# Hybrid SSM and attention layer: the attention stage's transfers in the written order

## Chip, cores and metric

The kernel runs on one core of one Trainium2 chip. The metric is the device time of one execution in microseconds. The engines are named as in the profile: PE is TensorE, DVE VectorE, ACT ScalarE, POOL GpSimd, SP SyncE (here it issues nearly all transfers).

## The reference

The reference is one layer: a pre-norm whose result feeds a state-space group and an attention group, an output projection, and a gated feed-forward part (2048 tokens of 1024 features, float32).

```python
h = rmsnorm(x, norm_mix_g[l])
proj = h @ w_in[l]                      # u_ssm (512) | q (512) | k (512) | v (512)
y_ssm = s5_mixer(u_ssm, ...)            # 32 groups of 16 channels, complex diagonal state of 64
y_att = chunked_attention(q, k, v, rel_bias)   # 8 heads of 64; own 64-token chunk and 8 before it
mixed = concatenate([rmsnorm(y_ssm, g_s), rmsnorm(y_att, g_a)])
x = x + mixed @ w_out[l]
h2 = rmsnorm(x, norm_ffn_g[l])
x = x + (silu(h2 @ w_gate[l]) * (h2 @ w_up[l])) @ w_down[l]
return rmsnorm(x, norm_final_g)
```

## The kernel before

A float32 product is made of three matmuls (`mm3`): each operand is split into a rounded high part (`hi`, `wh`) and the remainder (`lo`, `wl`), and hi by hi, hi by lo and lo by hi are added in PSUM. The stages follow one another: the SSM's input projection (`u_phase`, up to about 125 us), attention with the SSM as filler (about 143 to 731 us), mixing and output projection (from about 687 us), gate and up, and down (from about 1860 us).

The attention stage runs over 128 steps: 4 blocks of 512 tokens (`sb`), 4 pairs of heads, 2 heads, 4 query tiles. A step issues scores (`scores`: `sc`, with the mask tile `nb` added on DVE and the row minimum `mn`), the transposes of an earlier step (`transp`: `pt`, copied by ACT into `pth` and its remainder by DVE into `ptl`), the product with v at the end of a head (`pv_head`, `pv_scale`: `ya`, stored into `ya_s`), and then matmuls of "units", generators that are advanced a little in each step:

- `hT_unit` makes the normalised input tiles of a block, eight of them, q0 to q7. A tile `xt` is loaded into one of XB = 2 buffers, scaled on DVE, cast to `hi` by ACT and subtracted into `lo` by DVE (`low`). For blocks 1 to 3, q0 to q2 and q3 to q7 are two units, started 12 and 8 steps ahead of the block's first step.
- `qk_unit` and `v_unit` project q, k and v (`pf`). In block 0 their weights are loaded as `raw`, split into a hi and lo tile, and kept in DRAM (`keep_w`: `wss`). Later blocks load the split weights back (`w<-wss`, 1024 KB each) into WB = 3 buffers. q's two parts go to `q2h` and `q2l`, which are copied to the other half of the partitions by a transfer each. k's go to the right half of `k2`. The left half holds the keys of the block before, which were kept in DRAM (`ks`) and are loaded back.
- `ssm_unit` does four groups of SSM: U, Bst, Tm and Vm are loaded (18 transfers), products on PE, a scan on POOL, and y is stored in eight transfers (`y<-X`). Unit b starts at step 2 + 15 b.

A unit's loads are issued in the program two or three steps ahead of its matmuls. PE's order is the written one (`Ordered`). On the other engines a scheduler orders the instructions by its own priorities, except those issued through `Pinned` (`k.V`, `k.A`, `k.Q`), which it keeps in the order of the program among themselves on their engine. An instruction that waits on SP holds up all transfers that stand behind it. Tiles are named with a running number (`raw_2605`), which the order rows below show; in the profile the number is left out.

Of the kernel before, what the change touches and what calls it, by code (L numbers as in the profile page):

```python
# [78 lines left out]

class Pinned:  # L80


    def __init__(self, tc, eng):
        self.tc, self.eng = tc, eng

    def __getattr__(self, name):
        f = getattr(self.eng, name)
        return lambda *a, **b: self.tc.keep_in_program_order(f(*a, **b))


class K:
    def __init__(self, tc, io):
        self.tc, self.nc, self.io = tc, tc.nc, io
        self.n = 0
        self.te = Ordered(tc)
        self.ta = self.te if PINA else tc.nc.tensor
        self.V, self.A, self.Q = (Pinned(tc, e) for e in (tc.nc.vector, tc.nc.scalar, tc.nc.sync))
# [462 lines left out]
def ssm_unit(k, p, psum, S, b, eng):  # L560

    nc = k.nc
    F = GB * CH
    U = k.t(p, "U", [P, GB, NC])

    def load(out, in_):
        ins = nc.sync.dma_start(out, in_)
        if b == 0:
            k.tc.keep_in_program_order(ins)

    for j in range(L):
        load(U[j * CH : (j + 1) * CH], S["u"][b * F : (b + 1) * F, j, :].rearrange("(g c) t -> c g t", c=CH))
    gs = slice(GB * b, GB * b + GB)
    bst = k.t(p, "Bst", [P, GB, P])
    load(bst[:].rearrange("p g m -> p (g m)"), S["bst"][b // 2][:, (b % 2) * GB * P : (b % 2 + 1) * GB * P])
    tm = k.t(p, "Tm", [P, GB, P])
    for i in range(L):
        load(tm[i * CH : (i + 1) * CH], S["kt"].rearrange("c g a m -> c g (a m)")[:, gs, P - CH * i : 2 * P - CH * i])
    vm = k.t(p, "Vm", [P, GB, P])
    load(vm[:], S["v"].rearrange("q g c n m -> (c n) (q g) m")[:, gs, CH:])  # L580
    for _ in range(YL):
        yield

    X = k.t(p, "X", [P, 2, GP, NC])
    for q in range(GP):
        ps = k.t(psum, "pj", [P, 2, NC], bufs=2)
        for g2 in range(2):
            k.ta.matmul(ps[:, g2, :], bst[:, 2 * q + g2, :], U[:, 2 * q + g2, :], start=True, stop=True)
        for g2 in range(2):
            for c in range(2):  # L590
                nc.scalar.copy(X[g2 * NS : (g2 + 1) * NS, c, q, :], ps[c * NS : (c + 1) * NS, g2, :])  # L591
        yield

    a8 = S["a8"]
    qs = slice(GP * b, GP * b + GP)
    Xk = X[:].rearrange("p r q (k s) -> p r q k s", s=8)
    Xe = Xk[:, :, :, :, 7].rearrange("p r q (a b) -> p r q a b", b=8)

    def step(dst, src, e, n):

        ar = a8[:, 0, qs, (0, 7, 15)[e]].unsqueeze(1).to_broadcast([P, 2, GP]).unsqueeze(3).to_broadcast([P, 2, GP, n])
        aw = S["sw"][:, e, :, qs].unsqueeze(3).to_broadcast([P, 2, GP, n])
        t = k.t(p, "st1", [P, 2, GP, NC // 8])
        t2 = k.t(p, "st2", [P, 2, GP, NC // 8])
        eng.tensor_tensor(t[:, :, :, :n], src, ar, op=ALU.mult)  # L605
        eng.tensor_tensor(t2[:, :, :, :n], src[:, ::-1], aw, op=ALU.mult)
        eng.tensor_tensor(dst, dst, t[:, :, :, :n], op=ALU.add)
        eng.tensor_tensor(dst, dst, t2[:, :, :, :n], op=ALU.add)

    def carry(dst, end, i0, n):  # L610

        for c in range(2):
            for e in range(2):
                t = k.t(p, "fx", [P, GP, NC // 8, 7])[:, :, :n]
                pw = a8[:, c if e == 0 else 1 - c, qs, i0 : i0 + 7].unsqueeze(2).to_broadcast([P, GP, n, 7])
                eng.tensor_tensor(t, end[:, e].unsqueeze(3).to_broadcast([P, GP, n, 7]), pw, op=ALU.mult)
                eng.tensor_tensor(dst[:, c], dst[:, c], t, op=ALU.subtract if e == 1 and c == 0 else ALU.add)
            yield

    for s in range(1, 8):  # L620
        step(Xk[:, :, :, :, s], Xk[:, :, :, :, s - 1], 0, NC // 8)
        yield
    for b_ in range(1, 8):
        step(Xe[:, :, :, :, b_], Xe[:, :, :, :, b_ - 1], 1, 4)
        yield
    for a in range(1, 4):
        step(Xe[:, :, :, a : a + 1, 7], Xe[:, :, :, a - 1 : a, 7], 2, 1)
        yield
    yield from carry(Xe[:, :, :, 1:, :7], Xe[:, :, :, :3, 7], 8, 3)
    yield from carry(Xk[:, :, :, 1:, :7], Xk[:, :, :, : NC // 8 - 1, 7], 0, NC // 8 - 1)  # L630

    if b == 0:
        k.XG = k.t(p, "XG", [P, GB, NC])
        nc.gpsimd.memset(k.XG[:, :, 0:1], 0.0)
    XG = k.XG
    XGv = XG[:].rearrange("p (q g) c -> p q g c", g=2)
    for g2 in range(2):
        for c in range(2):
            eng.dma_start(XGv[c * NS : (c + 1) * NS, :, g2, 1:], X[g2 * NS : (g2 + 1) * NS, c, :, : NC - 1])
    for _ in range(YX):  # L640
        yield
    Y = k.t(p, "X", [P, GB, NC])
    for q in range(GP):
        ps = k.t(psum, "pj", [P, 2, NC], bufs=2)
        for g2 in range(2):
            g = 2 * q + g2
            k.ta.matmul(ps[:, g2, :], tm[:, g, :], U[:, g, :], start=True, stop=False)
            k.ta.matmul(ps[:, g2, :], vm[:, g, :], XG[:, g, :], start=False, stop=True)
        nc.scalar.copy(Y[:, 2 * q : 2 * q + 2, :], ps[:])
        if q == GP - 1:  # L650
            for j in range(L):
                nc.sync.dma_start(S["y"][b * F : (b + 1) * F, j, :].rearrange("(g c) t -> c g t", c=CH), Y[j * CH : (j + 1) * CH])
        yield


# [25 lines left out]
def att_phase(k, ident, S):  # L681
    tc, nc, io = k.tc, k.nc, k.io
    with ExitStack() as cx:
# [3 lines left out]
        def load_w(sb, n):  # L687

            w = k.t(aw, "w", [P, 2, 1024], F32R, bufs=WB)
            if sb == 0:  # L690
                raw = k.t(aw, "raw", [P, 1024], bufs=2)
                pin = n in (0, 4)
                (k.Q if pin else nc.sync).dma_start(raw[:], io["w_qk"][n] if n < 8 else io["w_v"][n - 8])
                split(k, w[:, 0], w[:, 1], raw[:], k.V if pin else k.wlo_eng, k.A if pin else None)
                keep[n] = w
            else:
                nc.sync.dma_start(f32(w[:]), S["ws"][n])
            return w[:, 0], w[:, 1]

        def keep_w(n):  # L700
            if n in keep:
                (k.Q if n in (0, 4) else nc.sync).dma_start(S["ws"][n], f32(keep.pop(n)[:]))

        def hT_unit(sb, q0=0, q1=KT):
            hi, lo = hT.setdefault(sb, ([], []))
            ts = slice(sb * SB, (sb + 1) * SB)
            xts = {}
            V, A, Q = (k.V, k.A, k.Q) if sb == 0 else (nc.vector, nc.scalar, nc.sync)

            def load(q):  # L710
                if q < q1:
# [9 lines left out]

            for q in range(q0, q1):
                yield
                load(q + ahead)
                xt = xts[q]
                for v, n in zip(hT[sb], ("hi", "lo")):
                    v.append(k.t(aw, f"{n}{q}x" if q < DB and sb % 2 else f"{n}{q}", [P, SB], F32R))
                V.scalar_tensor_tensor(xt[:], xt[:], k.gm[:, q : q + 1], S["rsn"][:, ts], op0=ALU.mult, op1=ALU.mult)
                A.copy(hi[q][:], xt[:])  # L729
                if sb == 0 and q:  # L730
                    low(q - 1)
                if sb or q == KT - 1:
                    low(q)
            yield

        def qk_unit(sb, pr):
# [5 lines left out]
            else:  # L742
                ts = [(k.t(aa, "q2h", [P, SB], F32R, bufs=3), k.t(aa, "q2l", [P, SB], F32R, bufs=3), k.t(aa, "k2", [P, 2 * SB], F32R, bufs=3)) for _ in range(2)]
            qk[sb, pr] = ts
            if sb > 0:
                for hh in range(2):
                    nc.sync.dma_start(f32(ts[hh][2][:, :SB]), S["k"][(sb - 1) % 2, 2 * pr + hh])
            both = (sb, pr) == (0, 0)
            pss = []
            for c in range(2):  # L750
# [13 lines left out]
                for hh in range(2):  # L764
# [3 lines left out]
                    if c == 0:  # L768
                        nc.scalar.activation(q2h[a, :], ps[a, :], AF.Copy, scale=-0.125)
                        nc.vector.scalar_tensor_tensor(q2l[a, :], ps[a, :], -0.125, f32(q2h[a, :]), op0=ALU.mult, op1=ALU.subtract)  # L770
                        nc.sync.dma_start(f32(q2h[o, :]), f32(q2h[a, :]))
                        nc.sync.dma_start(f32(q2l[o, :]), f32(q2l[a, :]))
                    else:
                        nc.scalar.copy(k2[a, -SB:], ps[a, :])
                        nc.vector.tensor_tensor(k2[o, -SB:], ps[a, :], f32(k2[a, -SB:]), op=ALU.subtract)
                        if sb < NSB - 1:
                            nc.sync.dma_start(S["k"][sb % 2, 2 * pr + hh], f32(k2[:, -SB:]))
                yield

        QK_N = 1 + 2 * KT  # L780
# [33 lines left out]

        def load_nb(h):
            nb = k.t(aa, "nb", [P, 640], bufs=2)
            nc.sync.dma_start(nb[:], S["nbm"][h])
            return nb

        def scores(st):  # L820
# [70 lines left out]
        def pv_scale(st):  # L891
# [4 lines left out]
            for i in range(4):  # L896
                k.ta.transpose(pb[:, i * P : (i + 1) * P], rb[:, i].rearrange("p h d -> p (h d)"), ident[:])
            nc.vector.tensor_tensor(ya[:], ya[:], pb[:], op=ALU.mult)
            nc.sync.dma_start(S["ya"][sb, pr * P : (pr + 1) * P, :], ya[:])

        st_head, yas, sums, rbs = {}, {}, {}, {}
        steps = [(sb, pr, hh, qp) for sb in range(NSB) for pr in range(4) for hh in range(2) for qp in range(4)]
# [43 lines left out]
        N = len(steps)  # L946
        for s in range(N + LAG + 2):
            if s == OPEN:
                aw.release()
                mix = mix_phase(k, S, lambda: k.t(pfs, "pf", [P, 512]))  # L950
                units += [Unit(islice(mix, MIX_N), MIX_N, GSTART, N + LAG, GSTART - OPEN)]
# [753 lines left out]
```

## Time and profile before

| | |
|---|---|
| median of 3 runs | 2314.3 us (2306.25 to 2315.94) |
| the profiled execution's own time | 2304.9 us |
| its span | 2303.1 us |
| its mean granted PE clock | 0.975 |
| PE busy in the span | 2183.8 us, 95% |
| transfers | 437 MB, 190 GB/s in the mean |

The profile is of one execution; its span runs from the first to the last instruction. A row of a timeline gives start, duration, engine, line, operation, and output and inputs; in brackets stand the idle time of the engine before it and what ended that. SPq is SP's queue, whose rows are transfers being issued; the row ends with the issue, and the transfer lands some microseconds later. The rows of transfers give the count, the KB of one and the median time from issue to landing.

### The profile page before, as it was taken

How to read it: one execution, taken by the hardware profiler on the slowest of the kernel's cores; microseconds unless marked ns; L12 is line 12 of the kernel's file. 1: busy time of each engine (PE TensorE's matmuls, PEld its weight loads, DVE VectorE, ACT ScalarE, POOL GpSimd, SP SyncE). 2: the span in 40 equal slices, each digit the busy share in tenths (PEclk: the TensorE clock that was granted, in tenths of full speed). 3: DMA queues.
4: the chain of work that ended last, by engine and by line, in shares of the span. 5: the costliest groups of instructions: out<-in, count | busy, mean ns of one | idle time of the engine just before them, and what ended most of it. 6: DMA issues, size and time to landing. Idle time of an engine off the chain costs nothing.

```text
span 2303.1 us, 30454 instructions
## 1 busy us (share of the span) xinstructions
PE 2183.8 (95%) x10568; PEld 1834.1 (80%) x10568; DVE 1487.8 (65%) x2286; ACT 1001.3 (43%) x1675; POOL 1061.0 (46%) x1245
## 2 busy tenths in 40 slices
PE   8978799999997899989999999999999999999997
PEld 6667688898986788778888887888888878888886
DVE  7845555656555756676775669766645376578676
ACT  6335555555557542343333335333333343344332
POOL 3416655455660433265555554555555314445442
PEclk9989999999998999999999999999999999999998
DMA  8788766766653534754554556555433287465552
GB/s 295 260 286 265 235 210 204 207 190 193 192 137 114 178 118 163 249 165 143 167 193 157 205 190 254 195 193 167 158 96 110 76 326 265 165 228 183 201 182 74
DMA packets 216370, 437.00 MB, mean 190 GB/s; under 512 B 27352, under 2 KB 58120, under 8 KB 209112
## 3 DMA queue, kind: packets, MB, share of 16 engines
q1 hardware_dynamic: 211352, 420.89, 55.0%
q0 software_dynamic: 4864, 14.17, 1.9%
q8 instruction: 83, 1.36, 0.2%
q14 instruction: 71, 0.58, 0.1%
HBM read 294.98 MB, written 132.15 MB: 185 GB/s over the span
## 4 chain that ended last, share of the span: by engine, by line
PE 59%; DVE 3%; DMA 1%; ACT 1%; issue 1%; POOL 1%; SPq 0%; DVEq 0%; ACTq 0%; POOLq 0%
PE X L74 20%; PE ps L74 18%; PE Y L74 10%; PE big L74 6%; PE W L74 5%; DVE acc L1575 1%; DMA lo<-hc 0%; DMA x<-xt 0%; DVE xt L1117 0%; DVE lo L166 0%; DVE hd L166 0%; POOL c L166 0%; ACT hi L165 0%; POOL sa L1125 0%; DMA gl<-x 0%
## 5 line engine op out<-in xcount | busy, mean ns | idle before, releaser
L74 PE MATMUL X<-hi,c 128*128 128x512 f32 x1408 | 452.2, 392 | 7.6 <-ACT u L1391 3.5
L74 PE MATMUL ps<-hd,hd 128*128 128x512 f32 (+1 forms) x1968 | 431.7, 381 | 3.9 <-DVE hd L166 3.7
L74 PEld LDWEIGHTS ps<-hd,hd 128*128 128x128 f32 x1968 | 358.8, 190 | 75.5 <-DVE hd L166 5.1
L166 POOL TENSOR_TENSOR c<-S,c 128x512 fp32r<-128x512 f32 x176 | 253.1, 1440 | 260.7 <-ACT c L165 258.8
L74 PEld LDWEIGHTS X<-hi,c 128*128 128x128 f32 x1408 | 265.8, 189 | 65.2 <-ACT u L1391 5.1
L74 PE MATMUL X<-lo,c 128*128 128x512 f32 x704 | 275.3, 391 | 0.0
L166 POOL TENSOR_TENSOR hd<-hd 128x1536 fp32r<-128x1536 f32 (+1 forms) x46 | 159.1, 3463 | 232.0 <-ACT hd L165 218.8
L166 POOL TENSOR_TENSOR c<-raw,c 128x512 fp32r<-128x512 f32 x132 | 189.0, 1432 | 137.5 <-ACT c L165 109.1
L165 ACT CAST hd<-hd 128x1536 fp32r<-128x1536 f32 (+1 forms) x106 | 147.4, 1393 | 219.4 <-DMA hd<-hq 134.5
L74 PE MATMUL Y<-hi,c 128*128 128x512 f32 x704 | 225.5, 391 | 4.8 <-DVE u L1395 4.8
L1521 DVE TENSOR_TENSOR acc<-acc,ps 128x512 f32<-128x512 f32 x196 | 129.2, 681 | 79.5 <-PE ps L74 79.1
L74 PE MATMUL big<-m,woh 128*128 128x512 f32 x512 | 165.4, 404 | 0.6 <-DVE m L166 0.4
L165 ACT CAST c<-S 128x512 fp32r<-128x512 f32 x176 | 109.5, 622 | 116.5 <-PE Y L74 59.1
L74 PE MATMUL pf<-hi,w 128*128 128x512 f32 x416 | 150.9, 415 | 9.4 <-ACT hi L729 5.8
L74 PEld LDWEIGHTS Y<-hi,c 128*128 128x128 f32 x704 | 132.6, 188 | 33.9 <-DVE u L1395 6.3
L74 PEld LDWEIGHTS X<-lo,c 128*128 128x128 f32 x704 | 133.0, 189 | 27.7
L1391 ACT COPY u<-X 128x512 f32<-128x512 f32 x132 | 77.1, 585 | 177.5 <-PE X L74 177.5
L846 DVE CUSTOM_DVE_ANT_0 s<-sc,nb 128x640 f32<-128x640 f32 (+4 forms) x128 | 94.4, 737 | 89.4 <-PE sc L74 85.9
L605 POOL TENSOR_TENSOR st<-X,a 128x128 f32<-128x128 f32 (+2 forms) x136 | 47.4, 349 | 220.0 <-ACT X L591 157.4
L165 ACT CAST c<-raw 128x512 fp32r<-128x512 f32 x132 | 82.1, 622 | 143.1 <-PE Y L74 80.3
L166 DVE TENSOR_TENSOR hd<-hd 128x1536 fp32r<-128x1536 f32 (+1 forms) x60 | 119.3, 1990 | 31.2 <-ACT hd L165 30.5
L74 PE MATMUL Y<-lo,c 128*128 128x512 f32 x352 | 137.2, 390 | 0.0
(462 smaller groups left out, 4644.2 us busy)
## 6 DMA issues: line engine op xcount, KB each, us to landing
w<-wss SPq DMA_DIRECT2D x36, 1024.0 KB, 5.5
hq<-g SPq DMA_DIRECT2D x140, 256.0 KB, 2.1
hd<-hq SPq DMA_DIRECT2D x42, 768.0 KB, 4.5
hd<-wc SPq DMA_DIRECT2D x42, 768.0 KB, 6.0
raw<-in_w_gate SPq DMA_DIRECT2D x44, 512.0 KB, 3.7
raw<-in_w_up SPq DMA_DIRECT2D x44, 512.0 KB, 4.1
wc<-px SPq DMA_DIRECT2D x66, 256.0 KB, 3.2
wss<-w SPq DMA_DIRECT2D x12, 1024.0 KB, 5.6
```

Of the source, the lines that this page charges most:

```text
L74: return self.tc.keep_in_program_order(self.tc.nc.tensor.matmul(*a, **b))
L165: (hi_eng or nc.scalar).copy(hi, raw)
L166: (lo_eng or nc.gpsimd).tensor_tensor(lo, raw, f32(hi), op=ALU.subtract)
L605: eng.tensor_tensor(t[:, :, :, :n], src, ar, op=ALU.mult)
L846: nc.vector.tensor_tensor_reduce(s[:, :nk].rearrange("p (a b) -> p a b", a=nch), ps[:, :nch, :half], hd.nb[:, nk - 1 :: -1].rearrange("p ( ...
L1391: nc.scalar.copy(u[:], ps[:])
L1521: V.tensor_tensor(a, a, ps[:], op=ALU.add)
L1575: nc.vector.scalar_tensor_tensor(v, v, k.go[:, i : i + 1], self.rs[:, : self.n], op0=ALU.mult, op1=ALU.mult)
```

## The change

In the attention stage every transfer of SP goes through `k.Q`, so that SP's order is the written one up to step 119 (OPEN), where `Pinned` is set free. Three things move in the written order besides: for blocks 1 to 3 the load of input tile q + 2 comes behind `low(q)`, the last use of its buffer; the kept keys are loaded behind the two q2 copies of their head, rather than at the unit's start; and they fill whole rows of `k2`. Since `Pinned` is free while the later stages are written, four copies of rows of w_down within DRAM (`wt`), which had been pinned in the gate stage, are left to the scheduler.

```diff
 class Pinned:
+    free = False
...
     def __getattr__(self, name):
         f = getattr(self.eng, name)
-        return lambda *a, **b: self.tc.keep_in_program_order(f(*a, **b))
+        return f if self.free else lambda *a, **b: self.tc.keep_in_program_order(f(*a, **b))
...
# ssm_unit: loads of U, Bst, Tm, Vm, and the stores of y
-        ins = nc.sync.dma_start(out, in_)
-        if b == 0:
-            k.tc.keep_in_program_order(ins)
+        k.Q.dma_start(out, in_)
...
-                nc.sync.dma_start(S["y"][b * F : (b + 1) * F, j, :].rearrange("(g c) t -> c g t", c=CH), Y[j * CH : (j + 1) * CH])
+                k.Q.dma_start(S["y"][b * F : (b + 1) * F, j, :].rearrange("(g c) t -> c g t", c=CH), Y[j * CH : (j + 1) * CH])
# load_w and keep_w
-                (k.Q if pin else nc.sync).dma_start(raw[:], io["w_qk"][n] if n < 8 else io["w_v"][n - 8])
+                k.Q.dma_start(raw[:], io["w_qk"][n] if n < 8 else io["w_v"][n - 8])
...
-                nc.sync.dma_start(f32(w[:]), S["ws"][n])
+                k.Q.dma_start(f32(w[:]), S["ws"][n])
...
-                (k.Q if n in (0, 4) else nc.sync).dma_start(S["ws"][n], f32(keep.pop(n)[:]))
+                k.Q.dma_start(S["ws"][n], f32(keep.pop(n)[:]))
# hT_unit
-            V, A, Q = (k.V, k.A, k.Q) if sb == 0 else (nc.vector, nc.scalar, nc.sync)
+            V, A, Q = (k.V, k.A, k.Q) if sb == 0 else (nc.vector, nc.scalar, k.Q)
...
-                load(q + ahead)
+                if sb == 0:
+                    load(q + ahead)
...
                 if sb or q == KT - 1:
                     low(q)
+                if sb:
+                    load(q + ahead)
# qk_unit
-            if sb > 0:
-                for hh in range(2):
-                    nc.sync.dma_start(f32(ts[hh][2][:, :SB]), S["k"][(sb - 1) % 2, 2 * pr + hh])
...
-                        nc.sync.dma_start(f32(q2h[o, :]), f32(q2h[a, :]))
-                        nc.sync.dma_start(f32(q2l[o, :]), f32(q2l[a, :]))
+                        k.Q.dma_start(f32(q2h[o, :]), f32(q2h[a, :]))
+                        k.Q.dma_start(f32(q2l[o, :]), f32(q2l[a, :]))
+                        if sb > 0:
+                            k.Q.dma_start(f32(k2[:, :SB]), S["k"][(sb - 1) % 2, 2 * pr + hh])
...
-                            nc.sync.dma_start(S["k"][sb % 2, 2 * pr + hh], f32(k2[:, -SB:]))
+                            k.Q.dma_start(S["k"][sb % 2, 2 * pr + hh], f32(k2[:, -SB:]))
# load_nb and pv_scale
-            nc.sync.dma_start(nb[:], S["nbm"][h])
+            k.Q.dma_start(nb[:], S["nbm"][h])
...
-            nc.sync.dma_start(S["ya"][sb, pr * P : (pr + 1) * P, :], ya[:])
+            k.Q.dma_start(S["ya"][sb, pr * P : (pr + 1) * P, :], ya[:])
# the step loop
             if s == OPEN:
+                Pinned.free = True
                 aw.release()
```

PE and POOL issue the same instructions in the same order as before, and from the mixing stage on so do the others, the `wt` copies apart. On SP, DVE and ACT the order within the attention stage differs. Three places show it.

SP at the start of the attention stage, before; `nb_1718` is the first mask tile of the steps, `w_1520` and `w_1525` are split weights that are stored:

```order
L777 DMA ks_68<-lo2x_1491 128x512
L702 DMA wss_75<-w_1520 128x2048
L702 DMA wss_75<-w_1525 128x2048
L817 DMA nb_1718<-nbms_69 128x640
L693 DMA raw_1762<-in_w_qk 128x1024
L693 DMA raw_1767<-in_w_qk 128x1024
L817 DMA nb_1805<-nbms_69 128x640
L714 DMA xt_2681<-in_xt 128x512
```

And after:

```order
L89 DMA ks_68<-lo2x_1491 128x512
L89 DMA nb_1718<-nbms_69 128x640
L89 DMA wss_75<-w_1520 128x2048
L89 DMA wss_75<-w_1525 128x2048
L89 DMA raw_1762<-in_w_qk 128x1024
L89 DMA raw_1767<-in_w_qk 128x1024
L89 DMA nb_1805<-nbms_69 128x640
L89 DMA wss_75<-w_1761 128x2048
L89 DMA U_1864<-u_64 16x4x256 x8
```

The mask tile stands ahead of the two stores, and the input tiles `xt_2681` and `xt_2683` of block 1 are no longer asked for here.

SP about steps 10 to 18 of block 0, before; `raw_2321` and `raw_2326` are the weights of the second v unit, `raw_2605` and `raw_2610` those of the last q/k unit, `X_2546` is the first SSM unit's output:

```order
L702 DMA wss_75<-w_2021 128x2048
L693 DMA raw_2321<-in_w_v 128x1024
L771 DMA q2h_2110<-q2h_2110 64x512
L772 DMA q2l_2111<-q2l_2111 64x512
L693 DMA raw_2326<-in_w_v 128x1024
```

and further down:

```order
L777 DMA ks_68<-k_552_2112 128x512
L777 DMA ks_68<-k_555_2115 128x512
L693 DMA raw_2605<-in_w_qk 128x1024
L693 DMA raw_2610<-in_w_qk 128x1024
L817 DMA nb_2636<-nbms_69 128x640
L714 DMA xt_2765<-in_xt 128x512
L714 DMA xt_2888<-in_xt 128x512
L702 DMA wss_75<-w_2604 128x2048
L714 DMA xt_2890<-in_xt 128x512
L567 DMA U_2614<-u_64 16x4x256
L652 DMA y_65<-X_2546 16x4x256 x8
L567 DMA U_2614<-u_64 16x4x256 x7
```

And after:

```order
L89 DMA wss_75<-w_2021 128x2048
L89 DMA ya_s_66<-ya_2047 128x512
L89 DMA raw_2321<-in_w_v 128x1024
L89 DMA raw_2326<-in_w_v 128x1024
L89 DMA ks_68<-k_552_2112 128x512
L89 DMA ks_68<-k_555_2115 128x512
L89 DMA nb_2432<-nbms_69 128x640
L89 DMA wss_75<-w_2320 128x2048
L89 DMA wss_75<-w_2325 128x2048
L89 DMA y_65<-X_2546 16x4x256 x8
L89 DMA raw_2605<-in_w_qk 128x1024
L89 DMA raw_2610<-in_w_qk 128x1024
```

The weights of v come behind a store of `ya`, and the last raw tiles come behind the eight stores of y, where they stood ahead of them.

DVE about steps 55 to 57, where block 2's first q/k unit begins, before; `xt_4714` and `xt_4721` are input tiles q5 and q6, `lo_1153` and `lo_1172` their remainders, `k_1073` and `k_1076` the keys of block 1's last pair of heads:

```order
L720 TENSOR_TENSOR lo_1150_4724<-xt_4632,hi_1149_4723 128x512
L865 TENSOR_TENSOR ptl_4612<-pt_4655,pth_4611 128x5x128
L875 RECIPROCAL rs_4834<-sm_4236 128x8
L728 SCALAR_TENSOR_TENSOR xt_4714<-xt_4714,g_mix_88,rsn_94 128x512
L775 TENSOR_TENSOR k_1073_4424<-pf_4545,k_1073_4424 64x512
L728 SCALAR_TENSOR_TENSOR xt_4721<-xt_4721,g_mix_88,rsn_94 128x512
L846 ISA s_4701,mn_4702<-sc_4696,nb_4579 128x640
L846 ISA mn_4702 128x1
L775 TENSOR_TENSOR k_1076_4427<-pf_4545,k_1076_4427 64x512
L865 TENSOR_TENSOR ptl_4612<-pt_4706,pth_4611 128x5x128
L720 TENSOR_TENSOR lo_1153_4731<-xt_4714,hi_1152_4730 128x512
L720 TENSOR_TENSOR lo_1172_4789<-xt_4721,hi_1171_4788 128x512
```

And after, where `xt_4630` and `xt_4632` are q3 and q4:

```order
L877 RECIPROCAL rs_4832<-sm_4236 128x8
L777 TENSOR_TENSOR k_1073_4424<-pf_4545,k_1073_4424 64x512
L777 TENSOR_TENSOR k_1076_4427<-pf_4545,k_1076_4427 64x512
L867 TENSOR_TENSOR ptl_4612<-pt_4706,pth_4611 128x5x128
L848 ISA s_4701,mn_4702<-sc_4696,nb_4579 128x640
L848 ISA mn_4702 128x1
L729 SCALAR_TENSOR_TENSOR xt_4630<-xt_4630,g_mix_88,rsn_94 128x512
L848 ISA s_4774,mn_4775<-sc_4769,nb_4579 128x640
L848 ISA mn_4775 128x1
L720 TENSOR_TENSOR lo_1146_4715<-xt_4630,hi_1145_4714 128x512
L729 SCALAR_TENSOR_TENSOR xt_4632<-xt_4632,g_mix_88,rsn_94 128x512
L867 TENSOR_TENSOR ptl_4612<-pt_4778,pth_4611 128x5x128
```

The two subtractions of k stand ahead of the input tiles, and the tiles' work is two tiles further back.

More of the change, by code (lines that the diff above doesn't have):

```diff
@@ L94, in __init__ @@
         self.n = 0
+        Pinned.free = False
         self.te = Ordered(tc)
```

## The prediction

> **What bounds the kernel now.** I read the page first: the engine line, then the chain of waits.
>
> ```profile
> PE 2183.8 (95%) x10568; PEld 1834.1 (80%) x10568; DVE 1487.8 (65%) x2286; ACT 1001.3 (43%) x1675; POOL 1061.0 (46%) x1245
> PE 59%; DVE 3%; DMA 1%; ACT 1%; issue 1%; POOL 1%; SPq 0%; DVEq 0%; ACTq 0%; POOLq 0%
> ```
>
> TensorE (PE) is busy for 2183.8 of 2303.1 us, and the chain that ended last runs mostly through it. The change alters neither the number of matmuls nor their order, so all it can do is add or remove holes between them. The windows by stage say how much hole there is where the change acts.
>
> ```profile
> 125.00:200.00 75.00, 59.49 (x336) 50.95 (x334) 32.04 (x69) 37.99 (x94) 26.65 (x63) 0.86 0.80 284
> 200.00:700.00 500.00, 466.41 (x2859) 418.16 (x2857) 289.63 (x544) 276.31 (x578) 270.46 (x651) 0.98 0.68 202
> ```
>
> In the 500 us of attention from 200 us on, PE is idle for 500 - 466.4 = 33.6 us. In the 75 us before that it is idle for 15.5 us, part of it in the prologue, and its clock is at 0.86. So a perfect change would win about 35 to 45 us, 2% at most. Next I read the PE timeline in that stretch and kept the stalls whose releaser stands on a queue that the change reorders (the bracket is the idle time before the row).
>
> ```profile
> 152.59 0.55 PE L74 MATMUL sc<-hi2x,hi0x 128*128 128x256 f32 x1 [3.34 <-DVE mn L846]
> 204.00 0.87 PE L77 MATMUL pt<-ident,s 128*128 128x128 f32 x3 [1.81 <-DVE ptl L865]
> 221.24 0.67 PE L74 MATMUL pj<-XG,Vm 128*128 128x256 f32 x2 [1.45 <-DMA XG<-X]
> 235.47 1.96 PE L74 MATMUL pj<-U,Bst 128*128 128x256 f32 x8 [1.14 <-DMA Tm<-kts]
> 261.95 0.79 PE L74 MATMUL pf<-hi,w 128*128 128x512 f32 x1 [3.45 <-ACT hi L729]
> 269.24 0.50 PE L74 MATMUL pf<-hi,w 128*128 128x512 f32 x1 [2.30 <-ACT hi L729]
> 307.25 1.97 PE L74 MATMUL pj<-U,Bst 128*128 128x256 f32 x8 [1.60 <-DMA U<-u]
> 399.22 0.42 PE L74 MATMUL sc<-k,q2h 128*128 128x320 f32 x1 [2.41 <-DVE k L775]
> 415.81 1.33 PE L77 MATMUL pt<-ident,s 128*128 128x128 f32 x5 [2.61 <-DVE ptl L865]
> 544.12 0.42 PE L74 MATMUL sc<-k,q2h 128*128 128x320 f32 x1 [2.85 <-DVE k L775]
> 642.88 2.70 PE L74 MATMUL pj<-U,Bst 128*128 128x256 f32 x8 [2.72 <-DMA U<-u]
> ```
>
> None of these is over 3.5 us. The reader is to see that they are many and small, and of two kinds: DVE work that PE waits for (mn, ptl, k), and operands that came late (hi, U, Tm, XG). SP's own waits say how full the queue is that feeds these operands.
>
> ```profile
> SPq L697 <- PE pf L74: 98.4, 25, 7.5
> SPq L747 <- PE sc L74: 46.1, 15, 6.5
> SPq L714 <- DVE lo L720: 22.3, 8, 5.9
> ```
>
> SP already stands for a free buffer of weights (L697, 98.4 us in all), of kept keys (L747) and of input tiles (L714). Whatever is queued behind such a wait is late.
>
> **The change, part by part.** It adds and removes no work. It sets SP's order to the written one, moves the loads of input tiles behind the last use of their buffer, and moves the loads of kept keys behind the two q2 copies.
>
> *What goes.* The key subtraction (k, L775) of blocks 2 and 3 no longer stands behind an input tile on DVE:
>
> ```profile
> 397.70 0.75 DVE L728 SCALAR_TENSOR_TENSOR xt<-xt,g_mix,rsn 128x512 f32<-128x512 f32 x1 [1.48 <-DMA xt<-in_xt]
> 398.48 0.69 DVE L775 TENSOR_TENSOR k<-pf,k 64x512 fp32r<-64x512 f32 x1
> ```
>
> DVE waits 1.48 us for a transfer and k sits behind it; in the new order both k come ahead of the tile. That takes the 2.41 and the 2.85. The ptl stall of 2.61 at 415.81, also behind tiles of that block, goes too. The mask tile nb_1718 stood behind the store of a weight:
>
> ```profile
> 144.45 0.71 SPq L817 DMA_DIRECT2D nb<-nbms  x1
> ```
>
> In the new order it is issued right at the start of the stage, 2 to 3 us sooner, and the 3.34 goes (mn is the reduction that reads it). The 1.81 had a weight's split on DVE ahead of ptl, which now comes later. The first SSM unit's stores and loads move forward, which takes the 1.45 and 1.14. Sum of waits: 2.41 + 2.85 + 2.61 + 3.34 + 1.81 + 1.45 + 1.14 = 15.6 us.
>
> A longer stall also slows what follows it:
>
> ```profile
> 545.52 0.63 PE L74 MATMUL pf<-lo0x,w 128*128 128x512 f32 x1
> 545.95 0.63 PE L74 MATMUL pf<-hi0x,w 128*128 128x512 f32 x1
> 548.49 0.40 PE L74 MATMUL pf<-hi2x,w 128*128 128x512 f32 x1
> 548.72 0.31 PE L74 MATMUL sc<-k,q2h 128*128 128x320 f32 x1
> ```
>
> After the 2.85 the matmuls start 0.43 us apart, and then 0.23 us apart. Eight of them (544.99 to 548.49) thus cost 8 x 0.2 = 1.6 us. I count this behind the three stalls of 2.61 to 3.34, which makes 4.8 us, and none behind the shorter ones. What goes is 20.4 us in all. The Trainium skill ("TensorE: Matmul & The Clock Gate", Part 1) lets the clock drop only after an idle window of about 3.4 us; none of these three waits is that long, so by it the 4.8 would be nothing and the sum below 4.8 us higher. The rows show the slow spacing after 2.85 us, so the trace decides.
>
> *What comes, in block 0.* Its weights arrive as raw tiles that must be split. In the old order those of v's second unit were asked for here:
>
> ```profile
> 187.98 0.98 SPq L693 DMA_DIRECT2D raw<-in_w_v  x1
> 196.39 0.58 SPq L693 DMA_DIRECT2D raw<-in_w_v  x1
> 202.31 0.32 SPq L899 DMA_DIRECT2D ya_s<-ya  x1
> raw<-in_w_v SPq DMA_DIRECT2D x2, 512.0 KB, 5.9
> raw<-in_w_v SPq DMA_DIRECT2D x4, 512.0 KB, 9.3
> 207.78 0.48 PE L74 MATMUL pf<-w,hi 128*128 128x256 f32 x2
> ```
>
> Now both come behind the store ya_s. Issued at 202.6 by the old clock, landing 5.9 later at 208.5, then split (an estimate of 1.2, two casts of 0.6 as in the tiles' row below) they are ready at 209.7 for the matmul of 207.78: 2 us late. With 9.3 us, the page's median for all four, it would be 5 to 6. I take 4. The last q/k unit's raw tiles, issued at 210.64, now come behind the y stores, which wait for the SSM unit:
>
> ```profile
> 210.64 1.87 SPq L693 DMA_DIRECT2D raw<-in_w_qk  x2
> 225.15 3.61 SPq L652 DMA_DIRECT2D y<-X  x8
> 231.35 0.48 PE L74 MATMUL pf<-hi,w 128*128 128x512 f32 x1
> raw<-in_w_qk SPq DMA_DIRECT2D x4, 512.0 KB, 6.1
> ```
>
> 225.15 + 3.61 = 228.8, landing 6.1 later at 234.9, the first half split at 235.5: 4 us late for 231.35 (3 to 5, as the y stores come earlier or not). Two tiles of block 1 now stand on DVE ahead of a ptl at step 21: one transfer wait like the 1.48 above, 1.7 with its own slack (0 to 3). The first splits each come one step later: 1.8 (0 to 3).
>
> *Input tiles.* q3 to q7 pass through two buffers. On DVE their work moves back by one to two steps in blocks 2 and 3, and in block 1 by three:
>
> ```profile
> xt<-in_xt SPq DMA_DIRECT2D x12, 256.0 KB, 4.6
> L729 ACT CAST hi<-xt x16: 607/620/622, 261.3 to 553.7; 128x512 fp32r<-128x512 f32 x16
> ```
>
> A round trip through a buffer is the transfer (4.6), the scaling (0.75, the xt row above), the cast (0.6) and lo (0.7, taken as the subtraction of k): 6.6 us, twice for five tiles. In block 1 the old order already lost 3.45 + 2.30 here, and the longer chain adds 3.5 (0 to 5). In block 2 it adds 4.5 and in block 3 5.0, each from 0 (the fillers of the same steps cover it) to 7 (one whole round trip on the path).
>
> *SSM loads.* U, Bst and Tm of units 2 to 4 and the last now come behind two weight loads that wait for a buffer. The stalls of 1.60 and 2.72 for U grow; I add 4 us over four units (0 to 8), less than half of a full 5 us wait at L697 per unit, since U was late there by under 3.
>
> *At no cost.* The four copies of w_down (wt) move from gate_up into the first 90 us:
>
> ```profile
> wt<-in_w_down SPq DMA_DIRECT2D x4, 512.0 KB, 8.2
> 60.00:80.00 20.00, 15.93 (x58) 11.59 (x57) 14.75 (x33) 7.19 (x13) 15.49 (x30) 0.83 0.95 331
> 80.00:90.00 10.00, 9.76 (x44) 7.44 (x43) 9.18 (x37) 6.47 (x10) 2.40 (x4) 1.00 0.40 117
> ```
>
> 2 MB at 331 GB/s are 6.3 us of transfer, in a stretch with the DMA at 0.95 followed by one at 0.40. I take 0 since the free share behind it, 0.6 of 10 us, holds them; without that cover it is 0 to 4. The later key loads land under sixteen and more matmuls; 0.
>
> **Sum.** 4 + 4 + 1.7 + 1.8 + 3.5 + 4.5 + 5 + 4 = 28.5 comes, 20.4 goes: +8 us. Against the profiled execution's 2304.9 that is 2313. The median of the runs is 2314.3, 9.4 above that execution, so a median after would be 2322. About 0.5% (11.6 us) is what a measurement of this kernel tells from no change.
>
> **Rivals.** *The loads are in time.* Everything in "goes" goes, but the fillers cover the tile chains and SSM loads (-17), while the two raw tiles and the rest stay at their low ends (5 of 11.5): 20.4 - 5 = 15 us faster, 2299. For it speaks SP's 98.4 us at L697, waiting that a planned order can shift; against it that the tiles' buffers stay two. It decides if hi of block 2 is ready when PE comes to it. *The tile chain is on the path whole.* In three blocks a round trip of 6.6 and the slow clock of 1.6 behind it: 24.6 instead of 13, so 2334. *Nothing.* PE's order stays, so each wait taken away is met again by the next late operand: 0 +- 4, 2314. The Trainium skill speaks against the change by its rule to issue a DMA early and wait late ("DMA: Bandwidth & Descriptors", Rules for kernel authors). By this rule the earlier asks of before were right, and the second rival's chain decides; the L747 row shows that asking early costs too, when the buffer is still in use.
>
> **How the numbers follow.** Forecast (a small loss, 2316 to 2328): 0.40. Whole chain, 2328 to 2340: 0.20. Nothing: 0.20. Loads in time: 0.20. All terms that come at their low ends give -15, all at their high ends 48 - 20.4 = +28, which is 2299 to 2342; not all will stand at one end at once, and the range 2300 to 2336 leaves out a tenth at each end. Beyond 11.6 us: the faster rival gives 0.20; slower is the second rival and the upper part of the forecast, 0.33; the rest, 0.47, is within 0.5%. The forecast's own range is 2316 to 2328.
>
> **What would show it.** PE's stalls for mn near 152 and for k near 399 and 544 gone; new stalls on w near 208 and 232; hi or lo as releaser near 262, 405 and 552, of 3 to 6 us each; U later by 1 to 2 us at 307 and 643. The stages from mixing on keep their lengths. I am wrong if the tiles land before PE asks, or if the w_down copies hold up the first 90 us.

## The result and the profile after

The changed kernel takes 2377.3 us (median of 5 runs) where the kernel before takes 2311.0; the ratio is 1.0285 (95% interval 1.0262 to 1.0309). It is 66 us slower. The profiled executions have spans of 2377.1 us against 2303.1, 74 us more, because the one profiled before was quicker than its median (2304.9 us). The page's row for the kept weights before, then the engine line and the same row after:

```profile
w<-wss SPq DMA_DIRECT2D x36, 1024.0 KB, 5.5
```

```profile
PE 2210.5 (93%) x10568; PEld 1849.7 (78%) x10568; DVE 1491.9 (63%) x2286; ACT 1003.1 (42%) x1675; POOL 1065.9 (45%) x1245
...
w<-wss SPq DMA_DIRECT2D x36, 1024.0 KB, 7.2
```

The count of matmuls is the same, but PE is busy for 26.7 us longer (2210.5 against 2183.8) and idle for 47.3 us longer. So about a third of these 74 us is matmuls at a lower clock. The windows by stage, before and then after, place all of it (a row has the window and its length, the busy time of PE, weight loads, DVE, ACT and POOL with their counts, the granted clock, the DMA share and GB/s):

```profile
200.00:731.00 531.00, 485.70 (x2940) 434.18 (x2939) 304.53 (x580) 297.33 (x603) 271.73 (x652) 0.96 0.66 197
...
1012.00:1861.00 849.00, 839.38 (x3691) 692.31 (x3692) 549.19 (x597) 320.11 (x551) 426.86 (x299) 1.00 0.49 168
```

```profile
200.00:802.00 602.00, 511.03 (x2928) 448.95 (x2927) 307.12 (x578) 299.46 (x603) 273.39 (x632) 0.91 0.57 179
...
1085.00:1935.00 850.00, 841.26 (x3692) 693.84 (x3693) 548.45 (x596) 319.75 (x550) 428.07 (x299) 1.00 0.48 165
```

The end of attention is at 731 before and at 802 after: 71 of the 74 us lie between 200 us and there, 25 of them PE busy and 46 PE idle. Its granted clock falls from 0.96 to 0.91 and DMA is less loaded than before. Gate and up keep their length. What PE waited for from 140 to 790 us, line by line (total us, times, longest), before:

```profile
PE pt L77 <- DVE ptl L865: 13.5, 10, 2.6
...
PE sc L74 <- DVE k L775: 6.8, 3, 2.9
...
PE pf L74 <- ACT hi L729: 5.8, 2, 3.5
PE sc L74 <- DVE mn L846: 5.6, 4, 3.3
...
PE pf L74 <- ACT w L165: 3.6, 1, 3.6
...
PE pj L74 <- DMA Tm<-kts: 1.8, 2, 1.1
```

After:

```profile
PE pf L74 <- DMA w<-wss: 19.5, 9, 6.0
PE sc L74 <- DVE mn L848: 15.2, 11, 2.2
PE pf L74 <- ACT hi L730: 13.1, 8, 3.3
PE pj L74 <- DMA Tm<-kts: 12.0, 4, 5.2
PE pf L74 <- ACT w L167: 11.5, 3, 4.9
...
PE pt L77 <- DVE ptl L867: 6.8, 6, 3.0
...
PE sc L74 <- DVE k L777: 4.0, 3, 1.4
```

The waits that were to go did shrink: ptl from 13.5 to 6.8, k from 6.8 to 4.0, and the wait of 3.34 us for the first mask tile to 1.22. But the largest row after, 19.5 us for kept weights (w from wss), has no row at all before. How this comes about is seen at the first v unit of block 1. SP's rows and PE's first matmul of that unit, before:

```profile
257.34 0.32 SPq L697 DMA_DIRECT2D w<-wss  x1
...
270.74 0.33 SPq L697 DMA_DIRECT2D w<-wss  x1
...
281.41 0.48 PE L74 MATMUL pf<-w,hi0x 128*128 128x256 f32 x2
```

After, with what stands ahead of the two loads:

```profile
277.09 0.42 SPq L89 DMA_DIRECT2D nb<-nbms  x1
284.65 0.47 SPq L89 DMA_DIRECT2D q2h<-q2h  x1
...
288.85 0.42 SPq L89 DMA_DIRECT2D ya_s<-ya  x1
289.32 1.86 SPq L89 DMA_DIRECT2D w<-wss  x2
...
298.17 0.79 PE L74 MATMUL pf<-w,hi0x 128*128 128x256 f32 x2 [3.84 <-DMA w<-wss]
```

Before, the two loads go out 24.1 and 10.7 us ahead of the matmul, each as soon as its buffer is free, past everything that waits for arithmetic. After, SP stands from 277.5 to 284.65 for a q2 copy that waits for ACT, then sends the rest in order, and both weights go out 9 us ahead, back to back. Over the 18 units of blocks 1 to 3 the median of that lead (first matmul of the unit minus the issue, from the timelines) falls from 23.6 to 7.4 us for the unit's first weight and from 11.2 to 6.3 for its second. A load takes 5.5 us to land before and 7.2 after (medians), so little or nothing is left over. SP's own waits from 140 to 790 us say the same. Those for a q2 copy, before:

```profile
SPq L771 <- ACT q2h L769: 29.1, 14, 6.1
```

After, with those for a product that frees a buffer:

```profile
SPq L89 <- ACT q2h L769: 102.6, 18, 12.8
SPq L89 <- PE pf L74: 42.7, 6, 17.1
```

SP's wait for such a product, 98.4 us before (L697 in the prediction), is 42.7 now; SP stands at the q2 copies in its place. The SSM unit of block 1 shows the second half of the loss:

```profile
311.88 3.60 SPq L89 DMA_DIRECT2D y<-X  x8
315.59 2.27 SPq L89 DMA_DIRECT2D w<-wss  x2
...
328.63 3.46 PE L74 MATMUL pj<-U,Bst 128*128 128x256 f32 x8 [5.23 <-DMA Tm<-kts]
```

These eight matmuls took 1.97 us before, behind a wait of 1.60 (the row of 307.25 in the prediction), and take 3.46 us after, behind one of 5.23: 1.5 us of slow clock come on top of 3.6 us of longer wait.

### The profile page after: what moved, and what is told of

It is laid out like the page before. It is cut to its first block, busy times and chain, and to the rows that moved or that the text cites. A ratio compares the mean times of both kernels' runs of the same rounds, so it can differ in the third digit from the quotient of the medians.

```text
span 2377.1 us, 30415 instructions
## 1 busy us (share of the span) xinstructions
PE 2210.5 (93%) x10568; PEld 1849.7 (78%) x10568; DVE 1491.9 (63%) x2286; ACT 1003.1 (42%) x1675; POOL 1065.9 (45%) x1245
## 4 chain that ended last, share of the span: by engine, by line
PE 55%; DVE 5%; DMA 2%; issue 1%; POOL 1%; ACT 1%; SPq 0%; DVEq 0%; ACTq 0%; POOLq 0%
PE X L74 18%; PE ps L74 18%; PE Y L74 9%; PE big L74 5%; PE W L74 4%; DMA lo<-hc 1%; DVE lo L168 1%; DVE acc L1578 1%; POOL c L168 0%; DMA x<-xt 0%; DVE xt L1120 0%; DVE g L1441 0%; DMA yr<-y 0%; DVE u L1398 0%; DVE hd L168 0%
```

## The experiments

Theory A: the written order itself costs, because it takes from SP's queue what the scheduler did there, asking for large operands far ahead of their written place. Theory B, from the prediction's second rival: the moved loads cost, above all the input tiles behind the last use of their two buffers. "Left to the scheduler" means `nc.sync` in place of `k.Q`, as in the kernel before.

**The two halves of the change.** First the moves alone, with `Pinned` set free at step 119 but every transfer issued as before:

```diff
-                load(q + ahead)
+                if sb == 0:
+                    load(q + ahead)
...
+                if sb:
+                    load(q + ahead)
...
-            if sb > 0:
-                for hh in range(2):
-                    nc.sync.dma_start(f32(ts[hh][2][:, :SB]), S["k"][(sb - 1) % 2, 2 * pr + hh])
...
+                        if sb > 0:
+                            nc.sync.dma_start(f32(k2[:, :SB]), S["k"][(sb - 1) % 2, 2 * pr + hh])
```

> Only the two moved loads (input tile q + 2 behind low(q), kept keys behind the q2 copies); every transfer is left to the scheduler as in the kernel before. Theory A (the written order itself is the loss: the scheduler used to ask for weights, SSM operands and raw tiles ahead of their written place, and now all stand behind waits): about as before, 2305 to 2320. Theory B (input tiles asked for late, through two buffers, are the loss, as the prediction's second rival has it): most of the 66 us is here, 2345 to 2375.

Measured: 2309.6, ratio 1.0001 (0.9984 to 1.0019). The moves by themselves do nothing: the scheduler put the loads nearly where they had been. Then the pins alone, with the loads at their old written places:

```diff
-                if sb == 0:
-                    load(q + ahead)
+                load(q + ahead)
...
-                if sb:
-                    load(q + ahead)
...
+            if sb > 0:
+                for hh in range(2):
+                    k.Q.dma_start(f32(ts[hh][2][:, :SB]), S["k"][(sb - 1) % 2, 2 * pr + hh])
...
-                        if sb > 0:
-                            k.Q.dma_start(f32(k2[:, :SB]), S["k"][(sb - 1) % 2, 2 * pr + hh])
```

> All transfers in the written order, but the two loads back at their old written places. Theory A: nearly all of the loss stays, 2360 to 2395. Theory B: 2310 to 2330.

Measured: 2377.3, ratio 1.0298 (1.0271 to 1.0325), the whole loss. Theory B falls as a cause of its own, and so does the idea that moving the loads mends what the order does.

**Kept weights.** The changed kernel with one line undone:

```diff
-                k.Q.dma_start(f32(w[:]), S["ws"][n])
+                nc.sync.dma_start(f32(w[:]), S["ws"][n])
```

> As the changed kernel, but the loads of kept weights of blocks 1 to 3 (w from wss) are left to the scheduler, which asks for them ahead of the q2 copies and y stores. Theory A: PE's waits for w from wss (19.5 us) go, and half as much again in slow clock: 2377 - 19.5 - 9 = 2348 (2340 to 2358). Theory B: within 8 us of the changed kernel, 2370 to 2380.

Measured: 2340.8, ratio 1.0139 (1.0116 to 1.0162), 36 us less than the changed kernel and 7 more than I had for it. Of the 38.3 us by which its span is shorter (2338.8), 20.4 are PE idle and 17.9 PE busy: I had put the clock at half of the wait, and it is nearly as much. Its engine line:

```profile
PE 2192.6 (94%) x10568; PEld 1840.0 (79%) x10568; DVE 1482.0 (63%) x2286; ACT 1003.2 (43%) x1675; POOL 1063.7 (45%) x1245
```

The row for w from wss is gone from PE's waits, and the median lead of a unit's first weight is back at 24.7 us. To see whether the weights' place costs by itself, I left everything large to the scheduler, first with the weights free too, then with the weights alone pinned among the small transfers:

```diff
# e6: the changed kernel with weights, raw tiles, their stores, SSM loads, y stores, input tiles through nc.sync
# e10: the same, but
-                nc.sync.dma_start(f32(w[:]), S["ws"][n])
+                k.Q.dma_start(f32(w[:]), S["ws"][n])
```

> As the changed kernel, but weights, raw tiles, stores of split weights, SSM loads, y stores and input tiles are left to the scheduler; in the written order stay only the q2 copies, the kept keys, the mask tiles and the stores of ya. Theory A: nothing large is late any more, 2305 to 2320. Rival (the small transfers' order costs by itself, since each q2 copy waits on ACT with the queue behind it): 2325 to 2345.

> As the kernel with small pins (2319), but the kept weights' loads are in the written order too, so that they come behind the q2 copies, kept keys and mask tiles. Theory A (the weights' place behind small transfers that wait costs by itself, whatever else is free): 2319 + 25 to + 40 = 2344 to 2359, with new waits of PE for w from wss of 15 to 25 us. Rival (the weights are late only because of the SSM unit's y stores and loads ahead of them, which are free here): 2319 to 2330.

Measured: 2319.0, ratio 1.0032 (1.0018 to 1.0047), and 2347.3, ratio 1.0159 (1.0139 to 1.0179). The weights cost 28 us with nothing but small transfers ahead of them (PE is 11.8 us longer busy, 2198.5 against 2186.7, and 18.8 us longer idle). PE's wait for them when they are pinned:

```profile
PE pf L74 <- DMA w<-wss: 17.7, 11, 6.8
```

So it does not take the y stores to make the weights late; the small transfers ahead of them, which wait for arithmetic, are enough. The lead of a unit's first weight is 7.8 us there (median of the same 18 units), as in the changed kernel.

**Asking earlier by hand.** PE's order is the same in both kernels:

```diff
# e7: three steps ahead for v and the last three q/k units
-            units += [ Unit(qk_unit(sb, 1), QK_N, g0 + C[2], g0 + C[3], 2, light=LIGHT),
+            units += [ Unit(qk_unit(sb, 1), QK_N, g0 + C[2], g0 + C[3], 3, light=LIGHT),
...
# e8: the first weight of a unit 4 (3) steps ahead, the second where its buffer comes free
-            ws = [load_w(sb, n) for n in (pr, 4 + pr)]
+            ws = [load_w(sb, pr)]
+            if sb:
+                yield
+            ws.append(load_w(sb, 4 + pr))
             yield
...
```

> All transfers in the written order, but the weights of the v unit and of the last three q/k units (and the second v unit) of each block are written one step earlier, three steps ahead of their matmuls. PE's order is the same. Theory A: the loads come ahead of more of the q2 copies and y stores, about half of the 36 us that freeing these loads gave: 2350 to 2362. Rival (two loads of 1024 KB back to back are slow by themselves, whenever asked): 2372 to 2380.

> All transfers in the written order, but in blocks 1 to 3 the two weights of a unit are written apart: the first four steps ahead (three for the first v unit), the second two steps ahead or at the unit's first step, where its buffer comes free. Theory A: as much as freeing the loads, about 2335 to 2348. Rival (only a scheduler that knows the waits can place them; by hand they block the queue elsewhere): 2355 to 2380.

Measured: 2368.8, ratio 1.0254 (1.0232 to 1.0277), and 2365.6, ratio 1.0249 (1.0225 to 1.0272). Both gave less than I expected, 9 and 12 us by the medians, and both intervals meet that of the changed kernel. PE's waits in the first and in the second:

```profile
PE pj L74 <- DMA Tm<-kts: 22.2, 6, 7.0
...
PE pf L74 <- DMA w<-wss: 13.5, 7, 5.2
```

```profile
PE sc L75 <- DVE mn L856: 19.7, 9, 6.5
...
PE pf L75 <- DMA w<-wss: 9.8, 5, 4.0
```

The wait for w falls, to 13.5 and 9.8, while that for the SSM operands (22.2 from 12.0, first kernel) or for the row minimum mn (19.7 from 15.2, second kernel) rises. In the first, one step earlier in the program brings a unit's first weight out only 1.4 us earlier (median lead 8.8 against 7.4) and its second not at all (6.3), since SP still stands at the q2 copies (99.0 us against 102.6), and SP's wait for a product that frees a buffer grows from 42.7 to 59.5 us: that a weight written earlier holds back what is now behind it is the likely reading. In the second it does not fit: the first weights do go out earlier (15.0 us), SP's wait for such a product falls to 10.5, and DVE waits no longer for mask tiles (5.5 us against 6.5). Why mn comes late there stays open.

**Block 0's weights and the SSM transfers.** From the kernel with free kept weights (e3) the raw loads and the stores of split weights go free as well (e5). From the changed kernel the SSM loads and y stores alone go free (e4).

```diff
# e5
-                k.Q.dma_start(raw[:], io["w_qk"][n] if n < 8 else io["w_v"][n - 8])
+                (k.Q if pin else nc.sync).dma_start(raw[:], io["w_qk"][n] if n < 8 else io["w_v"][n - 8])
...
-                k.Q.dma_start(S["ws"][n], f32(keep.pop(n)[:]))
+                (k.Q if n in (0, 4) else nc.sync).dma_start(S["ws"][n], f32(keep.pop(n)[:]))
# e4
-        k.Q.dma_start(out, in_)
+        ins = nc.sync.dma_start(out, in_)
+        if b == 0:
+            k.tc.keep_in_program_order(ins)
...
-                k.Q.dma_start(S["y"][b * F : (b + 1) * F, j, :].rearrange("(g c) t -> c g t", c=CH), Y[j * CH : (j + 1) * CH])
+                nc.sync.dma_start(S["y"][b * F : (b + 1) * F, j, :].rearrange("(g c) t -> c g t", c=CH), Y[j * CH : (j + 1) * CH])
```

> As the kernel with the kept weights' loads left to the scheduler (2341), and the raw weights of block 0 and the stores of split weights left to it too. Theory A (what stands late in the written order is the loss, part by part): PE's waits of 11.6 us for split weights (w, ACT) go, with some slow clock behind them: 2341 - 10 to - 15 = 2326 to 2331. Rival (the rest is the SSM loads and the tiles, and raw tiles matter little): 2336 to 2342.

> As the changed kernel, but the SSM units' loads and y stores are left to the scheduler. SP's stops of up to 17.3 us at a y store go, and with them PE's waits for Tm and the SSM operands (12 us) and part of those for w. Theory A: 2377 - 12 - 6 to - 12 = 2353 to 2360. Theory B: 2365 to 2380.

Measured for e5: 2333.9, ratio 1.0102 (1.0086 to 1.0118), 7 us better than e3, short of the 10 to 15. The row for split weights (w, ACT) in PE's waits of e3 and of e5:

```profile
PE pf L74 <- ACT w L167: 11.6, 3, 4.7
```

```profile
PE pf L74 <- ACT w L167: 3.6, 1, 3.6
```

Measured for e4: 2367.4, ratio 1.0256 (1.0227 to 1.0284), 10 us by the medians, though its interval meets that of the changed kernel.

**The input tiles.** They alone stay pinned beside the small transfers, at their new place (e9); and they alone go back to their old place, left to the scheduler, in the changed kernel (e12).

```diff
# e12 (e9: the reverse, on the kernel with small pins)
-            V, A, Q = (k.V, k.A, k.Q) if sb == 0 else (nc.vector, nc.scalar, k.Q)
+            V, A, Q = (k.V, k.A, k.Q) if sb == 0 else (nc.vector, nc.scalar, nc.sync)
...
-                if sb == 0:
-                    load(q + ahead)
+                load(q + ahead)
...
-                if sb:
-                    load(q + ahead)
```

> As the changed kernel, with the kept weights, block 0's raw and split weights, the SSM loads and the y stores left to the scheduler; the input tiles stay in the written order, which is the one difference from the kernel with small pins (2319). Theory A with the SSM loads as the rest: the 10 us that freeing them gave before come again, 2334 - 10 = 2322 to 2326, and the input tiles cost 3 to 7. Rival (the input tiles' place is the rest, as the prediction's chain of tiles has it): 2330 to 2335, no gain from the SSM loads.

> As the changed kernel, but the input tiles' loads of blocks 1 to 3 are back at their old place and left to the scheduler. With everything else free, putting them in the written order cost 14.6 us (2333.6 against 2319.0). If the parts add up: 2377 - 11 to - 17 = 2360 to 2366. If the late weights hide the late tiles (both are waited for in the first unit of a block): 2370 to 2377.

Measured for e9: 2333.6, ratio 1.0103 (1.0085 to 1.0122). It is 14.6 us over the kernel with small pins, and no better than e5, so once the weights are free the SSM transfers cost nothing to be seen and the tiles are the rest. The releaser hi, in e9 and in the kernel with small pins:

```profile
PE pf L74 <- ACT hi L732: 11.3, 5, 3.2
```

```profile
PE pf L74 <- ACT hi L731: 3.5, 2, 2.8
```

Measured for e12: 2363.7, ratio 1.0237 (1.0206 to 1.0268), 13.6 us under the changed kernel by the medians, with intervals that just meet: the parts add up here, and late weights do not hide late tiles.

**The mask tile.** The kernel with small pins has 0.3% left, with DVE's wait for the mask tile, 0.8 us in the kernel before, as its new row. The next kernel leaves `nb` to the scheduler too:

```diff
-            k.Q.dma_start(nb[:], S["nbm"][h])
+            nc.sync.dma_start(nb[:], S["nbm"][h])
```

> As the kernel with small pins (2319, 0.3% over before), but the mask tiles are left to the scheduler, so that only the q2 copies, the kept keys and the stores of ya stay in the written order. Theory A (what the small pins cost is the mask tile asked for late, for which DVE waits 7.0 us and PE, through mn, 15.7 instead of 5.6): back to before, 2308 to 2313. Rival (the q2 copies' order is the cost): 2316 to 2320.

Measured: 2313.0, ratio 1.0002 (0.9989 to 1.0015): no loss is left. DVE's wait for the mask tile with small pins, PE's wait for mn there, and PE's wait for mn in this run:

```profile
DVE s L847 <- DMA nb<-nbms: 7.0, 3, 3.3
...
PE sc L74 <- DVE mn L847: 15.7, 8, 4.6
```

```profile
PE sc L74 <- DVE mn L847: 5.2, 3, 3.3
```

So the order of the q2 copies, the kept keys and the stores of ya costs nothing to be seen; keeping behind them what is needed soon does cost.

**The part that won, alone.** The kernel before, with only the first mask tiles ahead of the first stores of split weights:

```diff
-            nc.sync.dma_start(nb[:], S["nbm"][h])
+            (nc.sync if k.n_nb > 1 else k.Q).dma_start(nb[:], S["nbm"][h])
+            k.n_nb += 1
# and k.Q for the stores of the first four split weights and the raw tiles of the next q/k unit
```

> The kernel before, but in block 0 the first two mask tiles, the stores of the first four split weights and the next unit's raw weights are in the written order, so that the first mask tile goes out ahead of two stores of 1024 KB. Theory A: the one part of the change that won stays won: PE's 3.3 us for the mask at step 1 falls to 1 to 2, and the slow clock behind it goes: 3 to 5 us faster than before, 2306 to 2308 where before is 2311. Rival (the next late operand takes it back within block 0): the same as before, within 1.5 us.

Measured: 2309.6, ratio 0.9996 (0.9986 to 1.0006), the rival's outcome. The wait at step 1 fell, to 1.88 us here, and the time did not.

```profile
152.03 0.35 PE L74 MATMUL sc<-hi2x,hi0x 128*128 128x256 f32 x1 [1.88 <-DVE mn L848]
```

No version that these runs point to beats the kernel before.

By ratios to the kernel before, the parts stack to most of the loss: mask tiles 0.3%, input tiles 0.7% (1.0103 to 1.0032), kept weights 1.3% (1.0159 to 1.0032), block 0's weights 0.4% (1.0139 to 1.0102), together 2.7% of 2.9%. What is left, 0.2%, is within the intervals; the SSM transfers, which gave 0.3% while the weights were late and nothing once they were free, may be it.

## Why the prediction was wrong

The forecast was +8 us within a range that ended at 2336; it measured +66 and 2377. By its own steps:

- *What goes* (20.4 us): half right. Of the seven stalls, 15.6 us, only about 4 were left (1.22 at the first mask tile and 1.31 at each of the two for k), and by step 2 PE was 4.1 us ahead of before, as the terms for the mask said. But the order that sent the first mask tile sooner sent many later ones late: DVE waited for one once before, 0.8 us, and seven times after, 6.5 us, and PE's row for mn grew by 9.6 us. I followed one tile of the 32. No run shows the 20.4 us as time: the one with the first mask tiles alone ahead shortened that wait and gained nothing clear of noise.
- *The kept weights*: the step that failed. They have no term in the sum. I read SP's 98.4 us at L697 as a queue that stands and holds others up, and in the "loads in time" rival as waiting that a planned order can win back. Those waits were the loads themselves standing at the head of the queue to go out the moment a buffer came free, some 24 and 11 us early. In the changed order the two loads of a unit stand next to each other behind q2 and ya, and I priced only the weights of block 0 and what stands behind the loads. SP's wait for a buffer did shrink, from 98.4 us to 42.7, but it moved to the q2 copies (29.1 to 102.6), and PE, which had not waited for a kept weight, waited 19.5 us. The missing term was 28 to 36 us.
- *Slow clock behind new stalls*: mis-sized. I counted 1.6 us behind three of the stalls that went and none behind those that came. PE was busy 26.7 us longer, and freeing the weights gave back 17.9 us of busy time for 20.4 of idle time. The Trainium skill ("TensorE: Matmul & The Clock Gate", Part 1) has the clock drop after an idle window of about 3.4 us. The trace before does not bear out that limit as one for a single stall: behind the waits of 2.61 us (at 415.81) and 2.85 us (at 544.12) matmuls of 512 columns start 0.43 us apart, where they start 0.23 us apart behind the 2.41 us at 399.22.
- *Block 0's raw tiles*: right in place, and near in size, for the two stalls. v's second unit waited 4.89 us (at 208.31, I had 4), the last q/k unit 2.99 (at 237.26, I had 4). With e5 the part is 7 us of time; my 4 + 4 + 1.8 was 9.8.
- *Input tiles*: the size was right, 13 forecast against 14.6 and 13.6 measured; PE's waits for hi and lo grew by 0.6, 3.6 and 4.8 us in blocks 1 to 3, where I had 3.5, 4.5 and 5. The cause was not the one I gave. With the loads at their old written place but kept in order (the pins alone) PE waits for hi as long, 13.5 us, and the time is the same: the order on SP costs, not the move behind the last use of the buffer. The second rival put them at 24.6, which they did not reach.
- *SSM loads*: 4 forecast; 10 by the medians with the weights late, 0 with them free. The cause was in the main another: with the kept weights' loads and block 0's weights free (e5), PE still waits 9.4 us for Tm, and 3.8 with the SSM transfers free as well (e9).

```profile
PE pj L74 <- DMA Tm<-kts: 9.4, 4, 3.7
```

```profile
PE pj L74 <- DMA Tm<-kts: 3.8, 3, 1.8
```

So most of it is these loads' own place behind the y stores. The two weight loads between y and U account for about 2 us of the 5.23 at 328.63: with the kept weights' loads free (e3), when one of them stands there, that wait is 2.99.

- *At no cost*: right for the copies of w_down. In the first 125 us PE was busy 111.15 us before and 111.20 after, and attention's first matmul starts 0.43 us later. Right for the moved key loads too: the changed kernel and the pins alone take the same time (2377.3 us both).

The Trainium skill's rule that I set against the change, to issue a transfer early and wait late ("DMA: Bandwidth & Descriptors", Rules for kernel authors), was the better guide to the sign, and the trace agrees: median leads of 23.6 and 11.2 us fell to 7.4 and 6.3, at median landings of 5.5 us before and 7.2 after.

## What to carry to other kernels

Before fixing the order of a queue, list for every large load how long before its use it goes out and how long it takes to land; a load whose lead is far over its landing time is a prefetch, and a wait in the queue at such a load is what keeps it early. In one in-order queue, a small store or copy that waits for arithmetic turns the loads written behind it into late ones, so keep in order only what is small and not needed soon, and let the loads pass. Writing them a few steps earlier by hand won 9 and 12 of the 66 us here. Price new stalls on TensorE at one and a half times to nearly twice their length where matmuls follow densely: in this stage 25 us of slower matmuls came with 46 us of idle time, and for the kept weights alone 17.9 with 20.4.

## What the runs showed of the hardware

Waits of 1 to 6 us, spread over the stage, cost in TensorE's clock six to nine tenths of what they cost in idle time: for the kept weights 17.9 us of longer matmuls beside 20.4 us of idle time where they were freed, 11.8 beside 18.8 where they were pinned among small transfers. A single wait of 2.61 us was followed by matmuls at about half their pace, one of 2.41 us was not.

The same 1024 KB load took 5.5 us to land in the kernel before, where most are issued alone, and 7.2 us in the changed kernel, where they go out in pairs, while the stage moved fewer bytes per second (179 against 197 GB/s). Where two were issued within 7 us of each other, the first took 6.0 us and the second 7.8 (medians of the 13 and 10 whose landing the trace of the changed kernel has). So it is mainly the second of a pair that is late. That it shares with its twin is the likely reason; no run isolates it.
